# V and gate columns of all sixteen heads by seven products, and the two head groups taking turns

## The chip, the cores and the metric

The kernel runs on one core of one Trainium2 chip. The metric is the device time of one execution in microseconds (us), taken as the median of several runs. Everything else is read from one execution recorded by the hardware profiler. The core's engines are TensorE (PE in the profile, with its weight loads as PEld), VectorE (DVE), ScalarE (ACT), GpSimd (POOL) and SyncE (SP). SP, ACT and POOL also issue transfers (DMAs), which 16 DMA engines carry out.

## What is computed

The reference is one layer of a decoder over 1024 tokens of width 2048, all in float32:

```python
hn = rmsnorm(h, norm_mix_g)
sb_q, sb_k, sb_v, sb_g, df_q, df_k, df_v, df_g = split(hn @ w_in)     # 8 blocks of 1024 columns
sb_out = stick_breaking_attention(sb_q, sb_k, sb_v)                   # 8 heads of 128, no positions
df_out = differential_attention(rope(df_q), rope(df_k), df_v, lam)    # 8 heads, two 64-wide q/k each
df_out = rmsnorm(df_out, subln_g) * (1 - lambda_init)                 # over each head's 128 values
mixed  = concat(sb_out * silu(sb_g), df_out * silu(df_g))
h = h + mixed @ w_out
h = h + sigmoid(rmsnorm(h, norm_ple_g) @ w_ple_gate) * (p @ w_ple_proj)
return rmsnorm(h, norm_final_g)
```

Stick-breaking weights are sigmoid(z) times a running product of (1 - sigmoid(z)) over the keys in between, so the kernel has a scan along the keys there. A differential head makes two causal softmaxes a and b and uses a - lam * b.

## The kernel before

**Precision and tiling.** Activations are kept with features on the partitions (128 at a time) and tokens along the free axis, in two halves of 512 tokens; half 1 is done before half 0 (tokens are stored in reverse order, so half 1's queries see half of the keys). A float32 matrix product is made of three matmuls on numbers split into a high and a low part (high x high, high x low, low x high). So each operand costs ACT one cast (the high part) and DVE one subtraction (the low part). One product of 128 x 128 weights with 128 x 512 activations is three matmuls.

**Seven products.** `class Seven` does a matrix product in 2 x 2 blocks (two column blocks by two halves of tokens) with seven block products in place of eight, in Winograd's form: operands A11, A12, A22 and the sums S1 to S4, weights and the differences T1 to T4 of them. It does so in two passes (`ph`) over the contraction, four k-tiles per block, so one product is 12 matmuls (`product`, lines 623 to 634) and one unit u is 2 x 7 products. Results of the first pass go to DRAM and are added to those of the second. Three stages use it: `gv` makes V and gate, `op` the output projection, and its continuation the embedding gate.

**Stage 1, V and gate.** In `gv` the two column blocks of a unit are V and gate of one stick-breaking head: 8 units. A first loop makes products A11 and A12 of the first pass for all units, then for each unit the other five, then pass 2 all seven. First-pass results lie in `vghalf_d`; in pass 2 SP loads them back (`r`, line 1030 and on), and DVE adds them (lines 1053, 1060, 1068, 1090); POOL stores the sums to `vg_d` through `vput` (line 831). The squares of x for the first norm are made beside it. `h_d` in DRAM receives x.

**Stages 2 and 3, attention.** For each half, heads come in the order `[8..15, 0..7]`: first the eight differential heads (`hd >= H`), then the eight stick-breaking ones. `unit(X)` makes 2 x 128 columns by direct products: 96 matmuls, streamed by `Stream`, with weights loaded by SP and split by `wprep` (`whi` at line 162, `wlo` at line 157). A stick-breaking head has one unit (q and k). A differential head has two: q and k, then V and gate. Low parts of stick-breaking heads are stored to `wlo_d` in half 1 and loaded in half 0; those of differential heads are computed in both.

**What sets the order.** TensorE, VectorE and ScalarE run exactly in the order in which the Python program emits their instructions. Work beside the units is a list of (time, function) in `Side`; the time is counted in ticks, and one tick is three matmuls of a unit, so a unit has 32 ticks. `attention(...)` returns such a list for a head, counted from the end of its unit: `weights(rb, c)` makes scores of a block of 128 query rows into PSUM and what follows on DVE and ACT at set delays (`DF` for differential heads), `turn` transposes the weights, `mix` multiplies them with V, `norm` is the differential heads' norm. POOL and SP take their DMAs in the program's order too.

**One block of scores.** For a differential head: a mask addition on DVE (line 326), the negated row maximum (line 364), the exponential with its row sum on ACT (line 370), a reciprocal (line 375), for the second softmax a scaling on ACT (line 378), and the difference (line 383). For a stick-breaking head: mask, two sigmoids (lines 342, 343), the scan (line 349), the product (line 354). Scores are made from q and k that were multiplied by the row scale 1/rms of their tokens (lines 1363, 1394, 1398). The gate's sigmoid of the first heads is built from exponentials and logarithms, since ScalarE holds one table of functions at a time, and loads another when a function of it is needed.

**Stage 4 on.** The output projection takes the heads in two passes: pass 0 contracts the differential heads, pass 1 the stick-breaking heads (`KA`, `mixed`). `last_steps` places the loads of its operands by ticks of the last head. Then come the embedding gate and the last norm.

## Time and profile before

| | |
|---|---|
| median of 3 runs | 2389.91 us (2388.15 to 2393.06) |
| span of the profiled execution | 2387.7 us; its own whole time is not given, the span is first to last instruction |
| granted TensorE clock, mean | 0.998 |
| busy share of PE, DVE, ACT, POOL | 99%, 78%, 50%, 10% |
| moved by DMA | 489.53 MB, 205 GB/s |

A row of groups names line, engine, operation, output <- inputs and shape, the count, then busy us in total, the mean ns of one, and the idle time of the engine just before, with what ended it. A row of waits names who waited for whom, the total us, the count and the longest. The time of a matmul in the trace is modelled, and neighbours overlap.

### The profile page before, as it was taken

The numbers are of one execution on the slowest core, as the hardware profiler recorded it, in microseconds if no ns is written. First come the engines' busy times: TensorE is split into PE (matmuls) and PEld (weight loads), VectorE is DVE, ScalarE is ACT, GpSimd is POOL, SyncE is SP. The second block draws the span as 40 slices with busy tenths as digits, with TensorE's granted clock in tenths as the row PEclk, the third lists the DMA queues.
The fourth block names the chain that finished last, engine by engine and source line by source line (L and its number), as shares of the span: only waits on it lengthen the run. The fifth ranks groups of instructions, "written<-read, shape, count | busy, mean of one in ns | idle before, by whom it ended". The sixth has DMA issues, their size and how long they took to land.

```text
span 2387.7 us, 32654 instructions
## 1 busy us (share of the span) xinstructions
PE 2360.2 (99%) x11318; PEld 1970.9 (83%) x11318; DVE 1863.9 (78%) x3245; ACT 1202.4 (50%) x2163; POOL 238.6 (10%) x367
## 2 busy tenths in 40 slices
PE   9999999999999999999999999999999999999998
PEld 7787878888888888888888888888788888888787
DVE  7887777777877778788888876767887987687787
ACT  6243345555556445555555566545643435532455
POOL 1211110000000000000000000110121121111000
PEclk9999999999999999999999999999999999999999
DMA  8887765444456777434444455666898889998965
GB/s 274 262 290 231 231 211 154 145 160 128 132 149 217 256 248 257 121 108 114 117 124 123 113 159 189 201 198 215 218 235 195 263 245 279 299 360 257 331 206 184
DMA packets 219413, 489.53 MB, mean 205 GB/s; under 512 B 24688, under 2 KB 36208, under 8 KB 219248
## 3 DMA queue, kind: packets, MB, share of 16 engines
q1 hardware_dynamic: 159872, 347.93, 44.4%
q0 software_dynamic: 42960, 109.86, 17.9%
q10 hardware_dynamic: 16416, 29.65, 3.6%
q8 instruction: 89, 1.46, 0.3%
q14 instruction: 76, 0.62, 0.1%
HBM read 336.09 MB, written 159.65 MB: 208 GB/s over the span
## 4 chain that ended last, share of the span: by engine, by line
PE 82%; issue 6%; DVE 5%; DMA 4%; ACT 2%; POOL 1%; SPq 0%; ACTq 0%; POOLq 0%; DVEq 0%
PE acc L240 14%; PE acc L242 14%; PE acc L241 14%; PE tp L415 2%; PE pbc L630 2%; PE pbc L628 2%; PE pbc L629 2%; PE z L319 1%; PE z L318 1%; PE pb L1730 1%; PE pb L1732 1%; PE pb L1731 1%; PE av L462 1%; PE pa L628 1%; PE pa L630 1%
## 5 line engine op out<-in xcount | busy, mean ns | idle before, releaser
L240 PE MATMUL acc<-xh,whi 128*128 128x512 f32 x1152 | 464.6, 403 | 0.0
L242 PE MATMUL acc<-xh,wlo 128*128 128x512 f32 x1152 | 450.8, 391 | 0.1
L241 PE MATMUL acc<-xl,whi 128*128 128x512 f32 x1152 | 450.3, 391 | 0.0
L162 ACT CAST whi<-wraw 128x1024 fp32r<-128x1024 f32 x192 | 201.7, 1050 | 123.7 <-PE acc L241 107.5
L242 PEld LDWEIGHTS acc<-xh,wlo 128*128 128x128 f32 x1152 | 216.2, 188 | 48.1 <-DVE wlo L157 0.5
L721 ACT CAST wpr<-T 128x512 fp32r<-128x512 f32 x144 | 87.8, 620 | 326.1 <-DVE T L680 245.5
L241 PEld LDWEIGHTS acc<-xl,whi 128*128 128x128 f32 x1152 | 217.2, 189 | 37.7 <-issue 0.2
L240 PEld LDWEIGHTS acc<-xh,whi 128*128 128x128 f32 x1152 | 216.8, 188 | 38.1 <-issue 0.2
L157 DVE TENSOR_TENSOR wlo<-wraw,whi 128x1024 fp32r<-128x1024 f32 x160 | 195.3, 1221 | 45.5 <-ACT whi L162 44.0
L434 ACT CAST awh<-tp 128x256 fp32r<-128x256 f32 (+1 forms) x160 | 80.6, 504 | 167.5 <-PE tp L415 166.9
L370 ACT ACTIVATE et<-z,mx 128x512 f32<-128x512 f32 (+7 forms) x128 | 94.7, 740 | 61.7 <-DVE mx L364 53.3
L721 ACT CAST wpr<-wraw 128x512 fp32r<-128x512 f32 x112 | 68.7, 615 | 112.1 <-DMA wraw<-tw_d 34.8
L439 DVE TENSOR_TENSOR awl<-tp,awh 128x256 fp32r<-128x256 f32 (+1 forms) x160 | 92.5, 578 | 41.7 <-ACT awh L434 41.5
L349 DVE TENSOR_TENSOR_SCAN st<-pt 128x511 f32<-128x511 f32 (+3 forms) x64 | 86.7, 1355 | 22.3 <-ACT pt L342 20.8
L735 DVE TENSOR_TENSOR wpr<-T,wpr 128x512 fp32r<-128x512 f32 x144 | 98.6, 685 | 3.6 <-ACT wpr L721 2.3
L364 DVE TENSOR_REDUCE mx<-z 128x1 f32<-128x512 f32 (+7 forms) x128 | 97.0, 758 | 4.4
L735 DVE TENSOR_TENSOR wpr<-wraw,wpr 128x512 fp32r<-128x512 f32 x112 | 75.9, 685 | 17.3 <-ACT wpr L721 17.2
L462 PE MATMUL av<-awl,v 128*128 128x256 f32 x256 | 73.2, 286 | 3.1 <-DVE awl L439 3.1
L240 PE MATMUL acc<-cA12h,whi 128*128 128x512 f32 x192 | 75.9, 395 | 0.0
L240 PE MATMUL acc<-cA11h,whi 128*128 128x512 f32 x192 | 75.6, 394 | 0.0
L241 PE MATMUL acc<-cA12l,whi 128*128 128x512 f32 x192 | 75.2, 392 | 0.0
L242 PE MATMUL acc<-cA12h,wlo 128*128 128x512 f32 x192 | 75.1, 391 | 0.0
(572 smaller groups left out, 6177.4 us busy)
## 6 DMA issues: line engine op xcount, KB each, us to landing
wraw<-w_in SPq DMA_DIRECT2D x192, 512.0 KB, 3.8
wraw<-w_gate SPq DMA_DIRECT2D x92, 256.0 KB, 5.7
wraw<-w_out SPq DMA_DIRECT2D x72, 256.0 KB, 4.5
wraw<-w_vg SPq DMA_DIRECT2D x71, 256.0 KB, 4.2
wlo_d<-wlo SPq DMA_DIRECT2D x32, 512.0 KB, 3.9
wlo<-wlo_d SPq DMA_DIRECT2D x32, 512.0 KB, 4.4
h_d<-hc POOLq DMA_DIRECT2D x56, 256.0 KB, 4.9
comb_d<-sg POOLq DMA_DIRECT2D x48, 256.0 KB, 7.3
```

The lines of the kernel that those rows point to most:

```text
L157: V.tensor_tensor(lo[:, o], raw[:, o], hi[:, o].bitcast(F32), op=ALU.subtract)
L162: side.later(1, lambda: A.copy(hi[:, o], raw[:, o]))
L240: T.matmul(acc[c], hi[:, k2, kh, c, :], xh, start=first, stop=False)
L241: T.matmul(acc[c], hi[:, k2, kh, c, :], xl, start=False, stop=False)
L242: T.matmul(acc[c], lo[:, k2, kh, c, :], xh, start=False, stop=last)
L349: V.tensor_tensor_scan(st[:, off + 1:nkey], pt[:, off:nkey - 1], pt[:, off:nkey - 1], initial=1.0, op0=ALU.mult, op1=ALU.bypass)
L364: V.reduce_max(mx, z[:, vw], axis=AX.X, negate=True)
L370: A.activation(et[:, vw], z[:, vw], AF.Exp, bias=mx[:, 0:1], accum_out=l)
L439: V.tensor_tensor(wl[:, o, :], tp[:, o, :], wh[:, o, :].bitcast(F32), op=ALU.subtract)
L462: T.matmul(av, vv[:, 0, blk % 4, :], wl, start=False, stop=last)
L721: A.copy(t[:, 0], src)
L735: V.tensor_tensor(t[:, 1], src, t[:, 0].bitcast(F32), op=ALU.subtract)
```

## The change

V and gate of the differential heads join stage 1: `gv` has 16 units (`NVG`), and `w_vg` and `w_in` are laid out on the host to match. Every head now has one direct unit, q and k. The heads alternate, differential j then stick-breaking j, in both halves, and the output projection's passes follow: pass 0 contracts heads 0 to 3 of either group, pass 1 heads 4 to 7.

In stage 1 the results of pass 2 are added to those of pass 1 in DRAM, by an accumulating DMA; the loads of the first-pass results and the DVE additions go, and A12 of pass 2 is copied by ACT. Squares are made at every other unit. Low parts of weights are stored and reloaded for all heads, in pieces as they are made.

In attention the starting times come from two constants (`TURN`, `LAG`). The differential head's V and gate are loaded like the others' (`load_vg`). Its q and k go to SBUF by an ACT copy, and the row scale is folded into the rotary tables (`scale_rope`). A stick-breaking head's q is not scaled any more; the row scale of queries enters as a per-row scale of the two sigmoids, from `rcol_of`, which transposes it by eight matmuls of one column. The scan writes over its input. For a differential head one custom DVE instruction adds the mask, scales and takes the row extreme. The two reciprocals of a pair are one instruction. The norm works once on 512 columns. The table of functions is loaded by explicit instructions: two per differential head. The gate is a plain sigmoid everywhere. K and V of half 1 are loaded nine ticks after the unit. The first masks become two wide tiles.

```diff
-ORDER1 = ORDER0 = [*range(8, 16), *range(8)]
+ORDER = [hd for j in range(8) for hd in (H + j, j)]
+NVG = 2 * H
+TURN = 76
+LAG = 15
+GAP = 4, 6
...
-            if keep is not None and half == 0:
+            if half == 0:
                 nc.sync.dma_start(lo.bitcast(F32), keep.bitcast(F32))
...
-            units = [(ap["w_in"][hd][i], half, hd) for half, order in ((1, ORDER1), (0, ORDER0)) for hd in order for i in range(1 if hd < H else 2)]
+            units = [(ap["w_in"][hd], half, hd) for half in (1, 0) for hd in ORDER]
...
-                    A.activation(pt[:, vw], z[:, vw], AF.Sigmoid, scale=-SB_SCALE)
-                    lastsig[0] = A.activation(bt[:, vw], z[:, vw], AF.Sigmoid, scale=SB_SCALE)
+                    A.activation(pt[:, off + 1:nkey], z[:, off:nkey - 1], AF.Sigmoid, scale=rcol[:, 0, rb:rb + 1])
+                    A.activation(bt[:, vw], z[:, vw], AF.Sigmoid, scale=rcol[:, 1, rb:rb + 1])
...
-                V.reduce_max(mx, z[:, vw], axis=AX.X, negate=True)
+                add = wide[0][:, 0:nkey - off]
+                if rb == 3:
+                    V.tensor_tensor(wide[1][:, 0:P], z[:, 2 * P:3 * P], add[:, 0:P], op=ALU.add)
+                    add = wide[1][:, 0:nkey - off]
+                V.tensor_tensor_reduce(z[:, vw], z[:, vw], add, -DF_SCALE, 3.0e38, ALU.add, ALU.min, mx)
...
+        gap = GAP[half]
+        if sb:
+            b = TURN + LAG - 64
+            ss, t0, t1, tv = [[b - 2 + 8 * rb] for rb in range(4)], b + 15, b + (36 if half else 32), 23
         else:
-            s0, s1, s2, t0 = [0, 2], [5, 8], [12, 15], 19
...
+            t0 = TURN - 32
+            ss = [[t0 - 20 + 8 * rb + 4 * c for c in range(2)] for rb in range(4)]
+            t1, tv = t0 + 17, t0 - 4
...
+            steps.append((t0 - 21.5, partial(A.preload_act_table_set, LOGS)))
+            steps.append((t0 + 12, partial(A.preload_act_table_set, SIGS)))
...
-        gv = Seven(lambda u, ph, k: ap["w_vg"][u, ph, k], H)
+        gv = Seven(lambda u, ph, k: ap["w_vg"][u, ph, k], NVG)
...
         def vput(o, ph, hf, blk, u):
-            G.dma_start((vg_d if ph else vghalf_d)[hf, blk, u], o)
+            G.dma_start(vg_d[hf, blk, u], o, **(dict(accum_op=ALU.add) if ph else {}))
...
-                r = {}
-                for e in ((1, 1), (1, 0), (0, 1), (0, 0)) if ph else ():
-                    r[e] = ev.tile([P, HALF], F32, name="hr", tag="xt", bufs=4)
-                    nc.sync.dma_start(r[e], vghalf_d[e + (u,)])
...
+        def rcol_of(hf):
+            ps = pp.tile([P, 4], F32, name="rcps", tag="t")
+            for j in range(4):
+                T.matmul(ps[:, j:j + 1], rstds[hf][:, j * P:j * P + P], ones[:, 0:1], start=True, stop=True)
...
+        def scale_rope(hf, cs):
+            V.tensor_tensor(cs, cs, rstds[hf].unsqueeze(1).to_broadcast([P, 2, HALF]), op=ALU.mult)
...
+                        A.copy(f, acc[c])
...
-                    vacc = two_accs()
-                    unit(X, acc=vacc)
```

More of the change, by code (lines that the diff above doesn't have):

```diff
@@ L286, in mixed, with attention @@
         G.dma_start(S4, t, accum_op=ALU.add)
-    def attention(at, pz, half, hd, q, qz, K, KL, VV, sg, vg):
+    def attention(at, pz, half, hd, q, qz, K, KL, VV, sg, vg, rcol):
         sb = hd < H
@@ L319, in scores @@
                     T.matmul(o, qz[:, c, rs], KL[:, ki, c0:], start=False, stop=True)
+            if not sb:
+                return z
             def masked():
-                mask = masks[:, 0 if sb else 1, :]
+                mask = masks
                 if rb == 3:
@@ L552, in attention @@
                 steps.append((t + gap * g, partial(turn, pr, g)))
-            steps.append((t + gap * n + (2 if sb and half and pr else 0), partial(mix, pr, n - 1)))
-            if not sb:
-                steps.append((t + gap * n + (7 if tight else NORM_LAT), partial(norm, pr)))
+            steps.append((t + gap * n, partial(mix, pr, n - 1)))
+        if not sb:
+            steps.append((t0 - 21.5, partial(A.preload_act_table_set, LOGS)))
+            steps.append((t0 + 12, partial(A.preload_act_table_set, SIGS)))
+            if half == 0 and hd == ORDER[-2]:
+                steps.append((t0 + 42.4, partial(A.preload_act_table_set, LOGS)))
+            steps.append((t0 + 44.5, norm))
         return steps
@@ L869, in some @@
                     todo.popleft()()
-        for u in range(0, H, 2):
+        for u in range(0, NVG, 2):
             aa = [pp.tile([P, HALF], F32, name="pa", tag="acc", bufs=2) for _ in range(2)]
@@ L1027, in _body @@
         for ph in range(2):
-            for u in range(H):
-                last = ph == 1 and u == H - 1
-                r = {}
-                for e in ((1, 1), (1, 0), (0, 1), (0, 0)) if ph else ():
-                    r[e] = ev.tile([P, HALF], F32, name="hr", tag="xt", bufs=4)
-                    nc.sync.dma_start(r[e], vghalf_d[e + (u,)])
+            for u in range(NVG):
+                last = ph == 1 and u == NVG - 1
                 early = ph == 0 and u in s1s
```

285 lines of the change are left out of this document (129 added, 156 removed).

## The prediction

> **What bounds the kernel now.** I read the page first (busy shares, slices, chain), then the busy time by stage, then the waits that TensorE (PE) had, then the groups by line for prices.
>
> ```profile
> span 2387.7 us, 32654 instructions
> PE 2360.2 (99%) x11318; PEld 1970.9 (83%) x11318; DVE 1863.9 (78%) x3245; ACT 1202.4 (50%) x2163; POOL 238.6 (10%) x367
> PE 82%; issue 6%; DVE 5%; DMA 4%; ACT 2%; POOL 1%; SPq 0%; ACTq 0%; POOLq 0%; DVEq 0%
> ...
> 200.00:300.00 100.00, 100.00 (x443) 82.68 (x442) 78.98 (x126) 33.14 (x60) 11.36 (x21) 1.00 0.73 234
> ...
> 0.00:325.00 325.00, 319.67 (x1381) 260.15 (x1382) 262.85 (x411) 137.47 (x239) 51.11 (x100) 1.00 0.80 260
> 325.00:740.00 415.00, 415.00 (x1971) 346.50 (x1970) 320.31 (x678) 224.47 (x445) 21.56 (x34) 1.00 0.49 150
> 740.00:955.00 215.00, 213.59 (x1068) 179.47 (x1067) 165.21 (x290) 110.45 (x218) 13.33 (x20) 1.00 0.74 246
> 955.00:1440.00 485.00, 484.50 (x2442) 410.03 (x2441) 391.49 (x719) 278.52 (x478) 34.02 (x48) 1.00 0.44 124
> 1440.00:1700.00 260.00, 254.77 (x1361) 216.59 (x1361) 183.84 (x270) 138.31 (x227) 27.43 (x36) 0.99 0.68 203
> ```
>
> In the window rows the columns are: length, then busy us and count of PE, weight loads, DVE, ACT, POOL; then granted clock, DMA share, GB/s. The five stages are: V and gate by seven products (to 325), half 1 of the differential heads (to 740), half 1 of the stick-breaking heads (to 955), half 0 of either (to 1440, to about 1700). PE is busy 2360.2 of 2387.7 us at a granted clock of 1.00, so only 27.5 us in all could be won by waiting less; anything larger must remove PE work. A matmul's own duration (391 to 403 ns) is not its price, because matmuls overlap: in the pure stretch 200 to 300, nothing but 128x512 products, 443 fill 100 us, so one costs 0.2257 us.
>
> ```profile
> PE av L462 <- DVE awl L439: 3.1, 4, 2.1
> PE pc L1730 <- DVE hc L1881: 3.1, 1, 3.1
> PE av L457 <- DVE lead L438: 2.7, 4, 1.0
> PE pbc L630 <- DVE wpr L735: 2.2, 4, 1.0
> ...
> L157 DVE TENSOR_TENSOR wlo<-wraw,whi 128x1024 fp32r<-128x1024 f32 x160 | 195.3, 1221 | 45.5 <-ACT whi L162 44.0
> L326 DVE TENSOR_TENSOR z<-z,masks 128x128 f32<-128x128 f32 x144 | 42.2, 293 | 39.0 <-PE z L316 24.7 <-PE z L319 13.8
> L364 DVE TENSOR_REDUCE mx<-z 128x1 f32<-128x1024 f32 x16 | 19.6, 1225 | 0.6
> L349 DVE TENSOR_TENSOR_SCAN st<-pt 128x1023 f32<-128x1023 f32 x8 | 18.3, 2289 | 5.5 <-ACT pt L342 5.5
> L1068 DVE TENSOR_TENSOR u<-u,hr 128x512 f32<-128x512 f32 x8 | 5.5, 692 | 0.3
> L513 DVE SCALAR_TENSOR_TENSOR rsub<-sqv,rsub 128x256 f32<-128x256 f32 x32 | 13.6, 425 | 1.1
> ...
> 1676.30 0.68 DVE L613 TENSOR_TENSOR cA12l<-cA12l,cA12h 128x512 fp32r<-128x512 f32 x1
> 1676.90 0.28 DVE L438 TENSOR_TENSOR lead<-tp,lead 128x128 fp32r<-128x128 f32 x1
> ```
>
> Every wait that PE has is short, and the engine named is nearly always DVE: low parts of attention weights (awl, lead), low parts of matrix weights (wpr). So DVE is the engine next in line. The last two rows show that a 0.68 us DVE operation lets the next one start after 0.60 us: back to back, 0.08 us comes off each.
>
> **PE work removed.** Before, each of the 8 differential heads has a second unit per half for V and gate: 2 x 96 = 192 matmuls a head. The seven-product scheme takes 2 x 7 x 12 = 168. Removed: 8 x 24 = 192 matmuls of 128x512, and 192 x 0.2257 = 43.3 us. All of it lies on the path, since PE is the path. In detail 1536 matmuls leave the attention stages (347 us) and 1344 enter the first stage (303 us). The norm matmuls go from 64 of 256 columns to 32 of 512, the same columns; 8 one-column matmuls for the transposed row scales are new, bounded by 8 x 0.2257 = 1.8 us, and I take 0.5.
>
> **The first stage gets longer, not denser.** It doubles from 8 to 16 units. Per unit of its second part, four DVE additions of a stored half (like L1068) go, because the sums are now accumulated by DMA; ACT gets one copy more. DVE has less to do per PE time than the 263 of 325 us shown, and the waits of the first row's 5.3 us (325 less 319.7) belong to its start and its change of operands, which stay single. I cost the denser part at nothing, hidden under PE; without that cover the four moves would be at most 16 x 0.6 us.
>
> The accumulating stores go out on POOL.
>
> ```profile
> L832 POOL DMA_DIRECT2D vg_d<-hc x32: 540/540/567, 177.1 to 323.5; - x32
> L284 POOL DMA_DIRECT2D comb_d<-sg x8: 875/878/892, 1072.0 to 1601.3; - x8
> L286 POOL DMA_DIRECT2D comb_d<-sg x16: 1176/1522/1551, 1073.1 to 1750.6; - x16
> vg_d<-hc POOLq DMA_DIRECT2D x32, 256.0 KB, 3.9
> comb_d<-sg POOLq DMA_DIRECT2D x48, 256.0 KB, 7.3
> ```
>
> A plain store of 256 KB takes POOL 0.54 us and lands after 3.9 us; an accumulating one took 0.88 to 1.52 us and landed after 7.3 us. Four per unit of 84 x 0.2257 = 19.0 us are 3.5 to 6.1 us of POOL, and the four buffers of the result tile come round once in 19 us, far behind 7.3. SP loses 4 loads per unit there. The cover holds: 0 us; what it costs if not is rival E.
>
> **Attention gets denser.** Half 1 took 630 us with 485.5 us of DVE (77%). After, PE needs 8 x 96 x 0.2257 = 173 us less, 457 us. DVE loses 32 low parts of weights (L157, 32 x 1.14 = 36 us), 80 mask additions of the differential heads (L326 and its like, 80 x 0.21 = 17 us), about 9 us by doing the sub-norm once over 512 columns rather than twice over 256 (12 operations like L513 become 6), and 24 scalings of q and k (24 x 0.6 = 14 us, now an ACT copy or folded into the activation); 64 accumulator reads and 16 small additions come in (about 8 us). 485 - 36 - 17 - 9 - 14 + 8 = 417 us in 457: 91%. Half 0: 745 us with 575 of DVE; after, 572 with 575 - 73 (64 low parts, the other 32 now come back by DMA) - 17 - 9 - 14 + 8 = 470: 82%. Averages would fit. But the order is uneven: counted from the instruction lists with durations of the same forms less 0.08, the slot of a stick-breaking unit in half 1 carries 26.0 us of DVE beside 26.9 us of PE, its neighbour 19.0 beside 27.2; in half 0 31.3 beside 35.0 and 22.3 beside 33.9; the one slot where the halves meet 32.4 beside 26.9. In the slots of 26.0 every bubble becomes lateness that the next slot repays.
>
> What that costs PE: a pair's transposes and products follow each other by 4 ticks in half 1 (differential heads had 6), about 3.3 us (a unit of 32 ticks in 26.9 us), and the steps between them, transposes, high copy, low subtraction, need about 1.9 us, 0.59 and 0.68 of it in rows shown here. So lateness under 1.4 us is free and the rest is a wait. The rows of such waits above are 0.8 us each (3.1/4, 2.7/4). I take 1 us for each of 8 pairs in half 1, 0.3 us for each in half 0, 4 us where the halves meet (32.4 + 1.4 - 26.9 less what the slack takes), and 2 us more at the end of attention, whose tail now runs 77 ticks into the output products where it ran 60: 16 us. Against it, the 7 us that PE waited in these stages (1375 less 1367.9) belong to places that no longer exist. Net +9, between -7 and +30.
>
> **Prices that the trace lacks.** The fused mask-scale-minimum operation of the differential heads, 128 of them over 73,728 columns, is new. Below it lies the plain reduction (1225 ns for 1024), above it the scan (2289 for 1023). I take the reduction, which also reads one PSUM tile once; the other end adds 73,728 x 1.04 ns = 77 us of DVE over the 16 pair slots, 2.7 us each in half 1 and 6.9 in half 0, still below PE (96% and 92%), about 1 us of wait more per pair: +16. Table loads rise from 19 to 43.
>
> ```profile
> 1467.23 0.59 ACT L434 CAST awh<-tp 128x512 fp32r<-128x512 f32 x1 [0.61 <-PE tp L415]
> 1467.84 1.28 ACT L507 ACT_TABLE_LOAD   x1
> 1469.14 0.48 ACT L507 ACTIVATE rsub<-msq,eps 128x256 f32<-128x256 f32 x1
> ```
>
> One load takes 1.28 us and its successor starts 1.30 us after it, so 24 more are 31 us of an ACT that in the pairs, counted as DVE was, is 60 to 64% busy; they are issued ahead of the block that needs them. 0 us on the path, at most 16 x 1.3 = 21 us if each held up a block. [...]
>
> SP's weight traffic in half 1 becomes that of the stick-breaking stage everywhere (low parts stored for all heads): that stage ran at a DMA share of 0.74 with 1.4 us of PE idle, so 0.
>
> **Sum.** 2387.7 - 43.3 + 0.5 + 9 = 2353.9 us of span. The median of the runs, 2389.91, lies 2.2 above this execution's span: 2356.
>
> **Rivals.**
> A, likeliest: as summed, 2356, own range 2340 to 2370. Its low end is -43.3 with the old waits gone and no new ones: 2340.
> B, part of the gain eaten: the fused operation at the scan's price (+16) or table loads on the path (up to +21): 2372 to 2386. For it: the new operation reads two operands and writes a third; ACT starts the chain of each block. Against: the averages stay below 97%.
> C, slower: DVE becomes the bound inside the pairs. DVE was idle for 23% of half 1 although PE never waited, because its operations wait for ACT and PE in turn. If that share of bubbles stayed, a pair would need (26.0 + 19.0)/0.77 = 58.4 us against 54.1 and, in half 0, 69.6 against 68.9: 8 x 5.0 = 40 us; slot by slot, without repayment, (33.8 - 26.9 + 40.6 - 35.0) x 8 = 100 us. With the 9 not counted twice, 2387 to 2447, say 2410. It turns slower from 43.3/16 = 2.7 us of PE wait per pair. Against: with more work ready, DVE's bubbles fill, and the longest such wait now is 2.1 us, once.
> E, the accumulating stores hold up the first stage: their four buffers come free late and PE waits for the result sums. At 1 us per unit it is +16, so 2372; it would have to be 2.7 us per unit to undo the gain. For it: landings of 7.3 us. Against: 540 ns as median and 567 as longest for POOL's stores, in a stage where DVE was busy 81% of the time. [...]
> D, no change by measurement: the mix that lands within 0.2% (4.8 us), which is about what a measurement of this kernel can tell.
>
> **How the numbers follow.** A 0.64, B 0.17, C 0.13, D 0.03, E 0.03. The time is A's. The range 2340 to 2388 leaves out most of C and a little below A. Faster: A, B and E, 0.84; same 0.03; slower 0.13.
>
> **What would show it.** PE's count down by about 200, its 128x512 products at 0.226 us apart as before; a first stage of about 620 us with PE at 98%; half 1 in about 460 us and half 0 in about 575 to 590. The fused operation near 1.2 us for 1024 columns (B if near 2.3). PE's waits: awl and lead summed under 25 us in the pairs (C if over 45). Table loads x43 with no wait of PE behind them. The prediction is wrong if PE's idle time is above 70 us in all, or if the first stage waits on the accumulated stores.

## The result, and the profile after

The changed kernel takes 2402.46 us (median of 4 runs, 2401.45 to 2408.58) against 2390.92 for the kernel before beside it (2388.15 to 2393.06): a ratio of 1.0058, 95% interval 1.0043 to 1.0073. It is slower by 0.6%, where 1.4% faster was forecast. The profiled execution has 2402.06 us with a span of 2400.2, 12.5 more than before's span. The lines of its page, and of its groups by line:

```profile
span 2400.2 us, 32458 instructions
PE 2331.9 (97%) x11110; PEld 1939.2 (81%) x11110; DVE 1805.8 (75%) x3171; ACT 1241.2 (52%) x2209; POOL 296.1 (12%) x439
...
L836 POOL DMA_DIRECT2D vg_d<-hc x128 | 89.1, 696 | 453.8 <-DVE hc L1026 261.4 <-DVE hc L1083 113.9 <-ACT hc L903 33.8
L372 DVE CUSTOM_DVE_ANT_0 z<-z,wide 128x512 f32<-128x512 f32 (+7 forms) x128 | 97.4, 761 | 7.1 <-PE z L324 6.0
```
```profile
L372 DVE CUSTOM_DVE_ANT_0 z<-z,wide 128x1024 f32<-128x1024 f32 x16 | 19.6, 1224 | 0.0
L213 ACT ACT_TABLE_LOAD x33 | 42.3, 1283 | 0.6
```

TensorE (PE) has its 208 matmuls less, but its idle time went from 27.5 to 68.3 us. Where it lies is seen in the busy time by stage, first the kernel before, then the changed one. The four stretches are half 1, the stretch where the halves meet, half 0, and the end of attention, which lies beside the first output products; columns as in the prediction's window rows.

```profile
324.00:917.00 593.00, 592.55 (x2859) 495.80 (x2858) 452.90 (x914) 311.48 (x617) 31.41 (x49) 1.00 0.56 177
917.00:962.00 45.00, 43.79 (x218) 36.25 (x216) 39.88 (x68) 27.65 (x56) 5.07 (x7) 1.00 0.77 258
962.00:1650.00 688.00, 685.26 (x3525) 581.69 (x3526) 529.61 (x917) 384.14 (x642) 54.97 (x75) 1.00 0.50 146
1650.00:1785.00 135.00, 131.03 (x653) 108.59 (x652) 107.60 (x167) 73.36 (x135) 20.46 (x25) 0.99 0.83 229
```
```profile
624.00:1065.00 441.00, 428.66 (x2107) 359.31 (x2106) 357.51 (x740) 272.36 (x531) 29.57 (x47) 0.99 0.76 249
1065.00:1110.00 45.00, 35.30 (x162) 28.53 (x160) 33.58 (x78) 31.18 (x62) 3.90 (x6) 0.92 0.89 282
1110.00:1636.00 526.00, 519.02 (x2759) 438.78 (x2759) 408.00 (x737) 353.47 (x584) 50.86 (x71) 1.00 0.67 195
1636.00:1771.00 135.00, 112.73 (x552) 90.85 (x553) 101.58 (x176) 80.69 (x147) 17.56 (x22) 0.95 0.66 178
```

Length less PE's busy time is PE's idle time. Before it was 0.5, 1.2, 2.7 and 4.0 us; after it is 12.3, 9.7, 7.0 and 22.3. The rest of the execution, the new first stage included, waits no more than it did. The granted clock is below 1.00 only behind waits, though not behind all of them: summed over the whole trace in steps of 2 us, (1 - clock) times PE's busy time is 3.4 us before and 11.2 after. So of the 12.5 us more, -42.8 are the products removed (the prediction's -43.3 + 0.5), +40.8 idle time, +7.8 clock. The 6.7 left over is about what the 34 further waits (58 after, 24 before) cost if each loses 0.2 us that the profile counts as busy. In the rows below the product after the wait starts 2.44 us behind the start of the last three transposes, for a wait of 1.95; in half 0 a product without a wait starts 0.24 us behind three such transposes. This last part is argued, not measured apart.

What PE waited for, after:

```profile
PE acc L240 <- DVE q L1381: 13.4, 8, 2.0
PE av L469 <- DVE lead L450: 10.5, 10, 2.6
PE z L324 <- DVE kl L1416: 7.2, 2, 6.1
PE tp L427 <- DVE et L392: 4.3, 8, 1.7
PE av L474 <- DVE awl L451: 4.1, 6, 1.2
PE msq L519 <- DVE awl L451: 2.4, 7, 0.9
PE pa L634 <- DVE wflo L1287: 2.4, 1, 2.4
PE pa L632 <- ACT wfhi L1284: 2.3, 1, 2.3
```

The largest is new: a unit's first product (L240) waits for the low part of q (L1381). The timeline of one such place:

```profile
725.83 0.69 DVE L530 TENSOR_TENSOR sg<-sg,avb 128x512 f32<-128x512 f32 x1
725.99 0.49 PE L427 MATMUL tp<-ident,bt 128*128 128x128 f32 x3
...
726.55 0.63 ACT L272 ACTIVATE neg<-sg 128x512 f32<-128x512 f32 x1 [2.62 <-DVE sg L530]
...
727.09 0.57 ACT L1385 CAST q<-acc 128x512 fp32r<-128x512 f32 x1
...
727.69 0.69 DVE L1381 TENSOR_TENSOR q<-acc,q 128x512 fp32r<-128x512 f32 x1 [0.50 <-ACT q L1385]
...
728.43 0.50 PE L240 MATMUL acc<-cA11h,whi 128*128 128x512 f32 x1 [1.95 <-DVE q L1381]
```

Read backwards: PE wants the sum buffer `acc`. It is held by the low part of q, which reads the sums in PSUM (`f = acc[0]`, L1373) and waits for the high copy of q on ScalarE (ACT). That copy stands in ACT's queue behind the negation of the finished differential head (L272), for which ACT waited 2.62 us, until VectorE (DVE) had done the last of the four operations of the sub-norm (L527 to L530). Before, one DVE operation read these sums into SBUF and the buffer was free.

### The profile page after: what moved, and what is told of

The parts are those of the page before. It is cut to its first block, busy times and chain, and to the rows that moved or that the text cites. A ratio compares the mean times of both kernels' runs of the same rounds, so it can differ in the third digit from the quotient of the medians.

```text
span 2400.2 us, 32458 instructions
## 1 busy us (share of the span) xinstructions
PE 2331.9 (97%) x11110; PEld 1939.2 (81%) x11110; DVE 1805.8 (75%) x3171; ACT 1241.2 (52%) x2209; POOL 296.1 (12%) x439
## 5 line engine op out<-in xcount | busy, mean ns | idle before, releaser
L240 PE MATMUL acc<-xh,whi 128*128 128x512 f32 x768 | 314.4, 409 | 1.8 <-DVE q L1381 1.7
L242 PE MATMUL acc<-xh,wlo 128*128 128x512 f32 x768 | 301.8, 393 | 1.4 <-DMA wlo<-wlo_d 0.9
L241 PE MATMUL acc<-xl,whi 128*128 128x512 f32 x768 | 301.1, 392 | 0.0
L242 PEld LDWEIGHTS acc<-xh,wlo 128*128 128x128 f32 x768 | 144.6, 188 | 34.6 <-DMA wlo<-wlo_d 1.3
L240 PEld LDWEIGHTS acc<-xh,whi 128*128 128x128 f32 x768 | 145.5, 190 | 27.0 <-ACT xh L1152 1.7
L241 PEld LDWEIGHTS acc<-xl,whi 128*128 128x128 f32 x768 | 145.4, 189 | 23.9 <-issue 0.2
L162 ACT CAST whi<-wraw 128x1024 fp32r<-128x1024 f32 x128 | 134.3, 1049 | 36.5 <-PE acc L241 19.8
L836 POOL DMA_DIRECT2D vg_d<-hc x128 | 89.1, 696 | 453.8 <-DVE hc L1026 261.4
L451 DVE TENSOR_TENSOR awl<-tp,awh 128x256 fp32r<-128x256 f32 (+1 forms) x160 | 92.5, 578 | 24.4 <-ACT awh L446 24.4
L372 DVE CUSTOM_DVE_ANT_0 z<-z,wide 128x512 f32<-128x512 f32 (+7 forms) x128 | 97.4, 761 | 7.1 <-PE z L324 6.0
L354 DVE TENSOR_TENSOR_SCAN pt<-pt 128x511 f32<-128x511 f32 (+3 forms) x64 | 86.7, 1354 | 15.8 <-ACT pt L347 15.3
L158 DVE TENSOR_TENSOR wlo<-wraw,whi 128x1024 fp32r<-128x1024 f32 x64 | 78.2, 1222 | 13.7 <-ACT whi L162 13.7
L472 PE MATMUL av<-awh,v 128*128 128x256 f32 x256 | 72.4, 283 | 0.2
L473 PE MATMUL av<-awh,v 128*128 128x256 f32 x256 | 72.4, 283 | 0.0
```

The costliest lines, as they stand in the source:

```text
L162: side.later(1, lambda: A.copy(hi[:, o], raw[:, o]))
L240: T.matmul(acc[c], hi[:, k2, kh, c, :], xh, start=first, stop=False)
L241: T.matmul(acc[c], hi[:, k2, kh, c, :], xl, start=False, stop=False)
L242: T.matmul(acc[c], lo[:, k2, kh, c, :], xh, start=False, stop=last)
L354: V.tensor_tensor_scan(pt[:, w], pt[:, w], pt[:, w], initial=1.0, op0=ALU.mult, op1=ALU.bypass)
L372: V.tensor_tensor_reduce(z[:, vw], z[:, vw], add, -DF_SCALE, 3.0e38, ALU.add, ALU.min, mx)
```

## The experiments

All edits are to the changed kernel. The table has for each run its median, the ratio to the kernel before on the same chip with its 95% interval, and PE's idle time (us) by place, read from window rows like those above.

| run | us | ratio | half 1 | meeting | half 0 | end of attention |
|---|---|---|---|---|---|---|
| before | 2390.92 | 1 | 0.5 | 1.2 | 2.7 | 4.0 |
| after | 2402.46 | 1.0058 (1.0043 to 1.0073) | 12.3 | 9.7 | 7.0 | 22.3 |
| e1 | 2394.91 | 1.0027 (1.0018 to 1.0037) | 8.6 | 7.9 | 7.0 | 21.6 |
| e2 | 2419.62 | 1.0131 (1.0116 to 1.0146) | 5.0 | 10.6 | 17.7 | 24.4 |
| e3 | 2402.05 | 1.0059 (1.0042 to 1.0076) | 11.8 | 9.1 | 6.9 | 19.8 |
| e4 | 2400.41 | 1.0049 (1.0034 to 1.0064) | 12.2 | 8.2 | 7.0 | 19.7 |
| e5 | 2403.39 | 1.0060 (1.0046 to 1.0073) | 6.0 | 10.4 | 7.4 | 22.8 |
| e6 | 2406.76 | 1.0075 (1.0062 to 1.0089) | 12.3 | 10.8 | 6.5 | 22.2 |
| e7 | 2408.60 | 1.0084 (1.0071 to 1.0098) | 12.5 | 8.1 | 8.1 | 24.5 |
| e8 | 2407.96 | 1.0080 (1.0066 to 1.0093) | 6.5 | 11.5 | 7.9 | 24.5 |
| e9 | 2402.22 | 1.0067 (1.0050 to 1.0083) | 9.3 | 10.0 | 6.7 | 23.2 |
| e10 | 2403.16 | 1.0066 (1.0051 to 1.0081) | 9.1 | 10.1 | 6.8 | 21.6 |
| e11 | 2403.79 | 1.0069 (1.0052 to 1.0086) | 12.3 | 9.5 | 6.5 | 21.6 |
| e12 | 2421.28 | 1.0135 (1.0120 to 1.0151) | 3.6 | 7.8 | 5.0 | 21.3 |
| e13 | 2390.03 | 1.0011 (1.0002 to 1.0020) | 0.8 | 8.3 | 6.7 | 20.7 |
| e14 | 2385.51 | 0.9986 (0.9977 to 0.9995) | 1.0 | 8.3 | 6.7 | 17.6 |
| e15 | 2387.81 | 0.9998 (0.9989 to 1.0007) | 0.5 | 10.1 | 8.4 | 19.2 |
| e16 | 2388.69 | 1.0002 (0.9993 to 1.0011) | 0.5 | 9.0 | 7.7 | 17.8 |
| e17 | 2378.20 | 0.9956 (0.9939 to 0.9973) | 0.9 | 2.0 | 7.8 | 19.7 |
| e18 | 2363.93 | 0.9894 (0.9879 to 0.9909) | 0.8 | 8.3 | 6.7 | 6.0 |

The theories: Q, work that waits stands in front of work that could run; C, DVE lacks room (the prediction's rival). Later ones are named where they come up.

**e1, the negation later**

```
-            A.activation(n, t, AF.Copy, scale=-1.0)      # half 1, at once
+            side.later(3, negated)                       # differential heads only
```

> The changed kernel with one ScalarE (ACT) instruction per pair of heads issued three ticks later: the negation of the finished differential head in half 1, which stands in ACT's queue directly in front of the high copy of the stick-breaking head's q. In the changed kernel TensorE (PE) waits 13.4 us in eight places for the low part of q, about 2 us per pair of half 1. Theory Q (queue order: work that waits stands in front of work that could run): half of this wait is ACT standing at the negation, so the eight waits fall from 13.4 to 4 to 9 us and the time by 6 to 12 us, to about 2393. Theory C (VectorE, DVE, has too little room in the pairs, the prediction's rival): the time saved is lost again at the next thing that DVE makes, total wait of PE in half 1 stays at 10 us or more, time within 3 us of 2402.

7.4 us were gained (1.0058 less 1.0027, times 2389). The eight waits for q fell from 13.4 to 8.3 us, as Q has it, and all waits of half 1 to 8.6.

**e2, the end of the sub-norm later in both halves**

```
-            side.later(4, step)
+            side.later(6, step)
```

> The changed kernel with the last four DVE operations of the sub-norm two ticks later, behind the low part of q rather than in front of it; the negation, which waits for them, goes with them. No work is left out or added. Theory Q: nothing that waits is in front of q any more, the waits for q in half 1 go from 12 us to under 3, the granted clock of the pairs returns to 1.00, and the time falls by 14 to 20 us, to about 2385. Theory C: DVE is as busy as before, so the wait moves to k, lead or awl; total wait of PE in half 1 stays above 9 us and the time above 2397.

Half 1 fell to 5.0 us, yet half 0 rose to 17.7 and the whole was 17 us slower. Q has the fall in half 1, C only the longer time; neither foresaw half 0, where PE now waits for lead (4.5 us), et (4.0) and two more results. That the four operations stand in front of these is argued.

**e3, less DVE work in half 1**

```
-                    V.tensor_tensor(vg[i], vg[i], rstd, op=ALU.mult)
+                    half or V.tensor_tensor(vg[i], vg[i], rstd, op=ALU.mult)
...
-                    V.tensor_tensor(sg, sg, vg[1], op=ALU.mult)
+                    half or V.tensor_tensor(sg, sg, vg[1], op=ALU.mult)
```

> The changed kernel without six DVE operations per pair in half 1: the scaling of v and of the gate by the row scale and the product of gate and sigmoid are left out there, so 6 x 0.6 = 3.6 us of about 45 us DVE work per pair. The order of everything else stays. Theory C (DVE's room): the relief is larger than the 2 us lost per pair, so PE's waits in half 1 go from 12.3 to under 4 us and the time falls by 12 us or more. Theory Q (order): the operations in front of q are all still there; the waits stay at 9 to 13 us and the time falls by 0 to 5 us.

DVE's busy time in half 1 fell from 357.5 to 334.1 us, yet half 1 still waited 11.8 us and the time did not move. DVE's load does not make the waits of half 1, so C is out for that place.

**e4, buffers of their own for the first output products**

```
-                    o = ftile()
+                    o = ev.tile([P, HALF], F32, name="hc", tag="xt", bufs=4) if u < 4 else ftile()
```

> The changed kernel with the results of the first eight output products in buffers of their own (four that are idle then) in place of the four that they share with v and the gate of the last two heads. Theory B (buffers): in the changed kernel ACT stood 4.2, 1.5 and 2.6 us for the store of an older result with weight and attention copies queued behind; without that, PE's waits between 1640 and 1770 us fall from 21.7 to 8 to 13 us and the time by 9 to 16 us, to about 2390. Rival C2 (DVE's room in the end of attention): only the two waits next to it go, the others stay or move; time falls by 0 to 5 us.

PE waits 2.6 us less in the end of attention. The gain of 2 us is within the intervals, which overlap, so it is not shown; it is in any case not the 9 to 16 us that were expected if the buffers held the end of attention.

**e5, the sub-norm's end behind k, in half 1 alone**

```
+            side.later(8 if half else 4, step)
```

> The changed kernel with the sub-norm's last four operations (and the negation that waits for them) four ticks later in half 1 alone, behind the reads of q and k, half 0 left as it was. In the run with two ticks in both halves, half 1 came out 8 us shorter and half 0 some 23 us longer. Theory Q (queue order in each half by itself): in half 1 no PE wait for q or for the low parts of the weights is left, PE's waits there fall from 12.3 to under 3 us, half 0 keeps its 7 us, and the time falls by 11 to 16 us, to about 2389. Theory S (any shift in one pair runs on into the next pairs): the waits move on, time within 5 us of 2402.

Half 1 ended 7 us earlier, but the time is the changed kernel's: in its profile half 0 and the output take some 4 us longer each, half 0 with the same waits and the output with 2.6 us more of them. That part was not explained. The four operations now delay a weight's low part (0.5 us in each pair) and lead (0.4).

**e6, e7, e8, the other two places, and all together**

```
-                            side.add([((5, 6, 13, 14)[i], load_x0(kt))])       # e6
+                            side.add([((8, 9, 18, 19)[i], load_x0(kt))])
-                    side.add([(27, partial(scale_rope, 0, cs))])
+                    side.add([(33, partial(scale_rope, 0, cs))])
-                weights_first(u, 28.5 + t, 43.0 + t)                            # e7, with e4
+                weights_first(u, 28.5 + t, 40.0 + t)
-                weights_first(u + 1, 36.5 + t, 47.5 + t)
+                weights_first(u + 1, 34.5 + t, 44.0 + t)
```

> The changed kernel with the splits of the new half's input (ACT cast, DVE low part, 16 of each) three to four ticks later, and the scaling of the rotation table six ticks later, where the halves meet; nothing left out. In the changed kernel PE waited 9.7 us there, 6.1 of it for the low part of k, in front of which DVE stood 3.0 us at a split whose ACT half was not done. Theory Q: with k's low part in front of the splits the waits fall from 9.7 to 3 to 6 us and with the clock that they cost the time by 5 to 9 us. Theory C (DVE has 32.4 us of work beside 26.9 of PE in this slot, so the room is what lacks): the waits stay at 8 us or more at whatever comes later, time within 2 us of 2402.

> The changed kernel with the buffers of the first output products apart (as in the run on the tail's buffers, which gained about 2 us) and the casts of the first output weights two to three ticks earlier. Theory Q: the waits for these weights (2.3 and 2.4 us) go, those for attention's low parts stay, PE's waits between 1640 and 1770 us go from 21.7 to 13 to 17 us and the time falls by 4 to 9 us. Theory C2 (DVE's room in the tail): an earlier cast pushes the low parts of attention back by as much; waits stay at 19 us or more, time falls by 1 to 3 us.

> The changed kernel with the edits of the last three runs together: sub-norm's end behind k in half 1, the new half's splits later, the first output products' buffers apart, their weights cast earlier. Theory Q: the gains add up, PE's idle time falls from 68 to 42 to 48 us, clock 0.996 or more, time 2374 to 2383, faster than the kernel before by 0.3 to 0.7%. Theory S (shifts run on) or C (DVE's room): 2392 or more.

All three missed what Q expected. In e6 the wait for k fell from 6.1 to 0.9 us, and waits for q (5.6) and et (4.3) took its place. In e7 the waits for the weights went and lead took 14.8 us where it had 7.2. In both the sum stayed or grew, as C has it for these places. e8 is no sum of gains.

**e9, e10, the sub-norm's end in the differential head's slot**

```
-            side.later(4, step)
+            side.later(24 if half else 4, step)        # and e1's negation, 4 ticks; e10: also e6
```

> The changed kernel with the last four operations of the sub-norm of half 1 moved twenty ticks on, into the differential head's slot (19 us of DVE work beside 27 of PE), behind the first low parts of attention there, and the negation four ticks behind them. The runs with two and four ticks freed q, but the four operations (2.9 us) then stood in front of a weight's low part and of lead. Theory L (what matters is whether a result that PE needs within some 3 us has other work in front of it, and the slot with room takes the four operations): PE's waits in half 1 fall from 12.3 to under 3 us, half 0 and the end stay, time falls by 10 to 15 us, to about 2390. Theory S (any shift runs on): waits in half 1 stay above 5 us, time above 2396.

> The run before with the later splits of the new half's input as well. Alone these splits only exchanged the wait for k (6.1 us) for waits for q and for the differential weights (5.6 and 4.3 us), which stood behind the sub-norm and the moved splits. Theory L: with the sub-norm out of this slot too, the waits where the halves meet fall from 9.7 to 3 to 6 us; time 4 to 8 us below the run before. Theory C (32.4 us of DVE work beside 26.9 of PE in this slot): the waits there stay at 8 us or more, whatever the order.

In both the negated part of a differential head is stored after its neighbour's part was added to the same sum, so that this part is missing from one of the four sums; the operations are the same. The wait for q is gone, but transposes now wait for the low part of v (4.7 us, six times) and products for k (3.6, five times): 9.3 us of the 12.3 are still there. Where the halves meet 10.1 us remain with the sub-norm out of the way, as C has it there.

**e11, the end of attention: low parts on POOL**

```
-                        V.tensor_tensor(lo, raw, hi.bitcast(F32), op=ALU.subtract)
+                        eng.tensor_tensor(lo, raw, hi.bitcast(F32), op=ALU.subtract)   # eng=G for the first operands
-                        V.tensor_tensor(lo[:, k], raw[:, k], hi[:, k].bitcast(F32), op=ALU.subtract)
+                        G.tensor_tensor(lo[:, k], raw[:, k], hi[:, k].bitcast(F32), op=ALU.subtract)
```

> The changed kernel with 36 low parts of the first output operands and weights (the 20 to 24 operand splits and 16 weight splits that lie in the end of attention) computed by GpSimd (POOL) in place of DVE; order and everything else as it was. This takes about 0.6 us each off DVE, over 20 us of the 97 that it is busy between 1640 and 1770 us. Theory C2 (DVE's room in the tail): the waits for attention's low parts, 6.6 and 4.1 us, and for the weights fall, PE's waits there go from 21.7 to under 12 us, time falls by 10 us or more. Theory L (order and delay, not room): the low parts of attention come no earlier than their transposes and copies let them; waits stay above 15 us. A third way: POOL takes far longer for one such operation than DVE (no row shows it), and PE then waits for the operands: time above 2410.

Nothing was gained, and I took that for L at first, wrongly, as e18 shows. The groups by line and the view of the tile pt (DVE's part, end of attention) say why; the first two rows are e11, the last is the same tile in e14:

```profile
L1287 POOL TENSOR_TENSOR wflo<-wraw,wfhi 128x512 fp32r<-128x512 f32 x16 | 24.9, 1626 | 1.1 <-ACT wfhi L1284 1.1
```
```profile
L354 DVE TENSOR_TENSOR_SCAN pt<-pt x5: 1490/2847/5599, 1644.1 to 1732.8; 128x639 f32<-128x639 f32 x2, 128x1023 f32<-128x1023 f32 x1, 128x895 f32<-128x895 f32 x1, 128x767 f32<-128x767 f32 x1
```
```profile
L354 DVE TENSOR_TENSOR_SCAN pt<-pt x5: 1489/1746/2282, 1627.7 to 1719.2; 128x639 f32<-128x639 f32 x2, 128x1023 f32<-128x1023 f32 x1, 128x895 f32<-128x895 f32 x1, 128x767 f32<-128x767 f32 x1
```

POOL takes 1.6 us where DVE takes 0.69, and DVE's scans take up to 5.6 us where they took up to 2.3. In the changed kernel's window of 135 us (1636 to 1771) DVE was busy 100.4 us with 43 operations less, 101.6 before the move: no room was made.

**e12, as much PE work put back**

```
-                    T.matmul(o, q[:, 0, rs], k[:, 0, c0:HALF], start=True, stop=False)
+                    for n in range(again(ki)):          # 3 in half 1; in half 0: 2 for the own keys, 1 for the others
+                        T.matmul(o, q[:, 0, rs], k[:, 0, c0:HALF], start=True, stop=n < again(ki) - 1)
```

> The changed kernel with PE work put back into the pairs and nothing else touched: the first product of each score block over the own keys is issued three times in half 1 and twice in half 0 (it starts its sum anew each time, so the result is the same). 18 and 9 products more per pair, of 512, 384 and 256 columns, 6912 and 3456 columns, at 0.2257 us per 512: 3.05 and 1.52 us, 8 x 4.57 = 36.6 us of PE work, against 43.3 us that the change removed. Theory P (PE is still the path, as the prediction had it): the time rises by all of it, 34 to 38 us, to about 2438. Theory L (in the pairs the path runs through delays of the chain PE, ACT, DVE, PE, and PE only waits less when it has more to do): PE's waits in half 1, where the halves meet and in half 0 (29 us) fall to under 15 and the time rises by 15 to 25 us only.

```profile
625.00:1075.00 450.00, 446.37 (x2227) 376.20 (x2226) 357.82 (x740) 272.82 (x531) 29.16 (x46) 1.00 0.75 243
```

36.6 us of products cost 18 us of time (1.0135 less 1.0058, times 2387), and half 1 waits 3.6 us where it waited 12.3. The three places together fall from 29.0 to 16.4 us, a little more than the 15 expected. So in the changed kernel's pairs about half of such PE work is cover for the chains of the other engines, not path.

**e13, e14, q copied out of PSUM**

```
-                            f = acc[0]
+                            f = f32t("qk"); A.copy(f, acc[0])       # with e1; e14: also e4
```

> The changed kernel with q of the stick-breaking heads copied by ACT from PSUM to SBUF first (16 copies of 0.57 us more on ACT), high copy and low part then from there, and the negation three ticks later as in the first run. DVE's order is the same; the sum buffer that the next unit needs is free after one ACT copy. Theory L: the waits for q in half 1 (11.7 us, 8.0 with the negation later) go to under 2 and do not come back elsewhere, since DVE's work has not moved; time 5 to 9 us below the first run's 2395, 2386 to 2390. Theory S (any shift runs on): the same sum of waits as in the first run, time 2393 to 2398.

> The run before with the first eight output products' results in buffers of their own, which alone gained 2 us. Theory L: 1 to 4 us below the run before, about 2385, at or just under the kernel before. Theory S: no better than the run before.

```profile
625.00:1048.00 423.00, 422.17 (x2087) 353.29 (x2087) 351.03 (x735) 274.10 (x537) 28.54 (x46) 1.00 0.78 256
```

Half 1 of e13 has 0.8 us of idle time at a clock of 1.00, with DVE as busy as before and one ACT operation more per pair. 11.2 us came back (1.0058 less 1.0011, times 2389): e1 alone had 7.4, and the copy adds 3.8 (the intervals of e1 and e13 just overlap, the waits of half 1 go from 8.6 to 0.8). No wait took the place of the old ones. The copy without the later negation was not run. The two edits move ACT's work and no operation of DVE, and their gain held. e14 is 0.14% below the kernel before: the interval leaves 1 out, but the gain is under the 0.2% that the prediction called a change.

**e15, e16, the halves' meeting and POOL again**

```
+                            side.add([((16, 17, 18, 19)[i], load_x0(kt))])     # e15, on e14
+                    side.add([(45, partial(scale_rope, 0, cs))])
```

e16 adds e11's first edit, for the operands alone.

> The run before (q copied out, tail buffers, 2385.5) with the sixteen splits of the new half's input moved to six to nine ticks ahead of the products that need them, behind the low parts of k, and the scaling of the rotation table 18 ticks later. Theory L (order; with q copied out by ACT the splits no longer hold a buffer that PE needs): the waits where the halves meet fall from 8.3 to 2 to 5 us, time by 4 to 9 us with the clock, to 2377 to 2382, faster than the kernel before by 0.2 to 0.4%. Theory C (32.4 us of DVE work beside 26.9 us of PE in this slot): the waits there stay at 7 us or more.

> The run before with the low parts of the first output operands (28) on POOL, which took 1.5 to 1.7 us each where DVE takes 0.69; the weights' low parts, whose wait took the gain in the earlier run on POOL (5.6 us), stay on DVE. Theory C2 (DVE's room in the tail): 18 us off DVE in and behind the tail, PE's waits there fall from 17.4 to under 10 us, time by 6 to 12 us. Theory L (delays of the chain, DVE waiting for ACT and ACT for PE): waits stay above 14 us, time falls by 0 to 4 us.

The wait for k went in e15, and waits for lead (4.2), the sum buffers (2.0) and, at the end of the stretch, et (4.2) came: 10.1 us. That was the third order of the same work with about the same sum. What DVE waited for in the stretch shows that this is not only a lack of room; the rows are the changed kernel and e15:

```profile
DVE xl L1153 <- ACT xh L1152: 5.2, 3, 3.0
DVE xl L1153 <- ACT xh L1152: 10.3, 7, 3.4
```

DVE stood still in front of the splits (xl) until ACT had made their casts (xh): 5.2 us of 45 in the changed kernel, 8.3 in e6, 10.3 in e15. So a later split left DVE idle while PE waited. e16 took 28 operations off DVE and DVE's busy time in the end of attention rose from e15's 105.8 to 110.2 us.

**e17, e18, DVE work left out**

```
-                V.scalar_tensor_tensor(lo, lo.bitcast(F32), gcol(kt), hi.bitcast(F32), op0=ALU.mult, op1=ALU.subtract)   # e17
-                        V.tensor_tensor(lo, raw, hi.bitcast(F32), op=ALU.subtract)                                       # e18, first operands
-                        V.tensor_tensor(lo[:, k], raw[:, k], hi[:, k].bitcast(F32), op=ALU.subtract)                     # e18, first weights
```

> The run with q copied out and tail buffers (2385.5) with the low parts of the new half's input left out (sixteen DVE operations of 0.7 us where the halves meet; the low operands then hold the loaded input itself), the order of all else as it was. Theory C for this place (32.4 us of DVE work beside 26.9 of PE): 11 us off DVE exceed what is lacking, the waits there fall from 8.3 to under 3 us, time by 5 to 10 us. Theory L: the waits stay above 6 us, as relief did nothing for the waits of q in half 1.

> The run with q copied out and tail buffers (2385.5) with the low parts of the first output operands (28) and of the first output weights (16) left out, 44 DVE operations of 0.69 us, some 27 of them between 1625 and 1760 us, with nothing given to another engine (the products read the loaded operand and the weights' high part in their place). Theory C2 (DVE's room at the end of attention): 18 us or more off DVE there, PE's waits fall from 17.4 to under 8 us, time by 9 to 15 us. Theory L (delays of the chain): only the wait for the weights (2.4) and part of lead go, waits stay above 12 us.

The rows are, in pairs, e14 and e17 where the halves meet, and e14 and e18 at the end of attention:

```profile
1049.00:1094.00 45.00, 36.71 (x174) 29.78 (x173) 36.26 (x82) 30.71 (x61) 4.60 (x7) 0.92 0.93 298
```
```profile
1040.00:1085.00 45.00, 42.98 (x215) 35.30 (x214) 33.09 (x78) 38.28 (x75) 4.64 (x7) 1.00 1.04 359
```
```profile
1621.00:1756.00 135.00, 117.36 (x578) 95.92 (x576) 105.56 (x182) 82.99 (x151) 20.03 (x24) 0.95 0.71 185
```
```profile
1617.00:1752.00 135.00, 129.04 (x661) 107.36 (x660) 96.34 (x163) 91.09 (x167) 22.57 (x27) 1.00 0.84 227
```

Without DVE's part of the sixteen splits the meeting waits 2.0 us for 8.3, and 7 us of time are gone (0.9986 less 0.9956). Without the 44 low parts the end of attention waits 6.0 us for 17.6, and 22 us are gone, where 9 to 15 were expected. The clock explains most of the surplus: its loss over the trace is 10.9 us in e14 and 3.4 in e18, and idle time fell by 12. Of these 12, only 2.4 are PE's own wait for a low part that is no longer made. Most of the rest are waits for attention's low parts, which are all still made. In the end of attention, first e14, then e18:

```profile
PE av L469 <- DVE lead L450: 6.6, 3, 2.6
PE av L474 <- DVE awl L451: 3.8, 6, 1.2
```
```profile
PE av L469 <- DVE lead L450: 3.9, 3, 2.4
PE av L474 <- DVE awl L451: 0.2, 1, 0.2
```

So at both places these DVE operations make PE wait. Whether it is by their own length or by DVE standing in front of them is not separated: e14's DVE stood 10.8 us of the end of attention at the same low parts for ACT's casts, and 4.1 us at the splits, and leaving the operations out takes away both. These two runs show which work it is and are no faster kernels, as the work is needed.

## Why the prediction was wrong

**PE work removed: right.** 208 matmuls are gone, the price held (442 of the 128x512 products fill the stretch from 500 to 600 us, 0.226 us each), and e12 shows what it missed: "All of it lies on the path" was true of the kernel before, not of the pairs after.

**First stage longer, not denser: right.** The first product of attention's units starts at 622.3 us for 322.3, 300 us later for 303 forecast, and the stage waits 3.2 us. The 696 ns of the row above are a mean of 64 plain stores (540 ns) and 64 accumulating ones, which take POOL 0.83 to 0.91 us each. None of PE's waits in the stage names them: rival E is refuted.

**Prices that the trace lacked: right.** The fused operation takes 1224 ns for 1024 columns, the plain reduction's 1225. There are 43 table loads (33 at L213 and the 10 that stood outside attention before too) of 1.28 us. In the kernel before ACT loads a table at 754.68, 757.71, 759.50 and 761.22 us, in front of a sigmoid, a logarithm, an exponential and a sigmoid again. None of PE's waits names a load as what ended it, and half 1 of e13, with all its loads, waits 0.8 us. Rival B is refuted for the fused operation and for the loads of half 1; whether a load lengthens one of the waits elsewhere was not tried.

**Attention gets denser: this step failed.** It took 16 us of new waits, net +9 with at most +30. Idle time rose by 40.8, and by place:
- Half 1, 8 us taken, 12.3 measured. The size is near, the mechanism is not. I reasoned from DVE's load in the slot of 26.0 us; e3 shows that load does not matter there, e1 and e13 that the release of the sum buffer does. The load was also put too high in the sum: 417 of 457 us (91%), where the prediction's own slots give 45.0 of 54.1 per pair (83%) and the changed kernel has 357.5 of 441 (81%). The edit `f = acc[0]` was in the diff, and the prediction counted it as a scaling saved. It made the release of the buffer the third step of a chain rather than the first.
- The halves' meeting, 4 us taken, 9.7 measured: the place and the work were right (e17), the size off, and the mechanism is right at most in part. The prediction had more DVE work than PE work there (32.4 us beside 26.9). But DVE was idle for 11.4 of the 45 us, 5.2 of them in front of a split for ACT's cast, a wait that the prediction's sum of durations leaves out.
- Half 0, 2.4 us taken, 7.0 measured, about 0.9 for each pair. e12 brings it to 5.0; no run took its cause apart.
- The end of attention, 2 us taken, 22.3 measured. I counted 17 ticks more of tail, not that attention of both last heads now lies beside the 44 low parts of the output's first operands and weights, on a DVE already 80% busy there (107.6 of 135 us before). e18 shows that these low parts make PE wait; how much of it is their length and how much the waiting for their casts stays open.

**A term was missing: the clock.** The sum priced a wait at its length. Waits also cost 7.8 us in lower granted clock, and in the end of attention a microsecond of waiting cost nearly two (e18: 12 of idle, 22 of time).

**The rivals.** The time fell into C's range (2387 to 2447). That is luck in the main: C's 40 to 100 us all lay inside the pairs, most of them in half 1, and the pairs waited only 19.3 us (12.3 and 7.0), those of half 1 by another mechanism. Where the halves meet and in the end of attention DVE's work does make PE wait, but C had no term for the end of attention, and a DVE without room is not shown there, as it was idle for a quarter of both stretches. The sign that I gave for C, awl and lead above 45 us, would have missed it: those are 17 us (10.5 + 4.1 + 2.4), and the rest of the waits stands against q, k, et and the output's first weights. The bound "wrong if PE idle is above 70" was all but reached, at 68.3.

## What to carry to other kernels

Products removed from a busy TensorE are worth their time only as long as the other engines' chains stay shorter than the work that is left (here 42.8 us of products went and 40.8 us of idle time came). When an edit makes a later step read PSUM in place of an earlier one, price the release of that buffer as a step of PE's own path (here 13.4 us of waits in eight places), with all that stands in front of each link in its engine's queue. A wait that only moves when work is reordered is not cured by order: leave the work out to see whether it is the cause, and read whether the busy engine works or stands still in front of it (here DVE stood 5 to 10 us at splits whose casts ACT had not made). A wait that relief does not touch tells of something held: free it with an engine that has room. Here a later negation and one copy per pair, both on ACT, gave back 11 us, and six reorderings (e2, e5, e6, e7, e9, e15) nothing.

## What the runs showed of the hardware

**The clock after a short wait.** Windows of 2 us of the changed kernel, behind two of the six waits for q of half 1, each of 1.95 to 1.97 us:

```profile
728.00:730.00 2.00, 1.57 (x6) 1.43 (x7) 1.21 (x4) 1.00 (x4) 0.00 (x0) 0.87 0.96 364
730.00:732.00 2.00, 2.00 (x6) 1.53 (x5) 1.48 (x4) 1.95 (x5) 0.00 (x0) 0.50 0.85 227
732.00:734.00 2.00, 2.00 (x8) 1.60 (x8) 2.00 (x5) 0.67 (x2) 0.68 (x1) 0.78 0.65 178
734.00:736.00 2.00, 2.00 (x13) 1.79 (x12) 1.75 (x5) 0.25 (x2) 0.00 (x0) 1.00 1.18 420
...
788.00:790.00 2.00, 2.00 (x10) 1.68 (x10) 0.69 (x4) 1.37 (x4) 0.00 (x0) 1.00 1.00 344
```

After the first, which ends at 728.4, the granted clock is half for about 3.4 us: read in windows of 0.25 us it is 0.50 in all thirteen from 729.50 to 732.75, 0.96 and 0.71 in the two beside them, and 1.00 around these. After the second, which ends at 787.7, it stays at 1.00. Two of the six waits of this kind (those that end at 728.4 and 845.4) were followed by a half clock, and the one of 6.1 us (which ends at 1075.7). Why these and not the others is not shown.

**POOL beside DVE.** In e11 POOL made low parts of the first output operands and weights, in 1.5 to 1.8 us each as the mean of a form. In the rows above DVE's five scans at the end of attention took 1490 to 5599 ns in e11, with a median of 2847; in e14 the same five forms took 1489 to 2282, median 1746, and in the changed kernel 1490 to 2283, median 1747. The six products behind them (`bt`, L358) took up to 2044 ns in e11 and up to 1218 in the other two. DVE was busy 100.4 us of the 135 from 1636 to 1771 us with 43 operations less, for 101.6 in the changed kernel. What held these operations up was not taken apart.
